# Skip path of a hybrid SSD and attention layer: from the output projection into the attention lanes, through a ring of row tiles; seven staging tiles for weight rows; POOL takes more of the splits

## The chip, the cores and the metric

The kernel runs on one core of a Trainium2 chip. The metric is the time of one execution on the device in microseconds (us), as a median of runs. A profile is one further execution, recorded by the hardware, and gives every instruction with its start and end.

The engines are named as in the profile: PE (TensorE, matmuls; PEld are its weight loads), DVE (VectorE), ACT (ScalarE), POOL (GpSimd), and SP (SyncE), whose queue issues the DMAs here.

## The reference, cut to what matters

One encoder layer on a sequence of 1024 rows of 1024 numbers. In the reference's own terms:

```python
h = layer_norm(x, ln_emb_g, ln_emb_b)
z, xbc, dt_f, dt_b, q, k, v, g = split(h @ w_in)
y_ssm = rms_norm(bidirectional_ssd(silu(conv(xbc)), dt_f, dt_b) * silu(z))
y_att = rms_norm(diff_attention(q, k, v)) * 0.8 * silu(g)      # 8 heads, 2 softmax maps each
mix = concat(y_ssm, y_att) @ w_out                             # 2048 -> 1024
out = layer_norm(alpha * h + mix, ln_g, ln_b)
```

The skip path is the term `alpha * h`. With the mean and the spread of each row of x already known from the first normalisation, it is computed from x again: `(x - mean) * rstd * (alpha * ln_emb_g) + alpha * ln_emb_b`.

## The kernel before

All float32 products are made on PE from halves: a value is split into a rounded high part (a copy on ACT) and a rest (a subtraction on DVE or POOL), and three matmuls take the place of one (high by high, high by low, low by high). Tiles with names in `h` and `l` are such halves: `oh`/`ol` and `or` hold rows of w_out, `oyh`/`oyl` rows of the concatenated y, `whi`/`wlo` columns of w_in, `wh`/`wl` the attention map transposed, `vh`/`vl` the values.

The program is written out by a small planner (`Loom`). Each piece of work is a generator, a *lane*, with a rank in the table `LANES`. At every step the planner takes, of the lanes whose condition holds, the one with the earliest modelled time, then the lowest rank, and at the same rank the one that was added first. PE keeps the order so written; on the other engines the framework places the instructions by the same program order and by what they wait for. Each engine, and the queue of SP, then runs its instructions strictly in its order: what stands behind a waiting instruction waits too.

The stages are: the first normalisation and projections; the SSD groups; eight attention heads (`scores`, `combine`, `values`, `finish`), into which the projections of the next head are filled by the lane `fill`; the last head (head 7), into which the first output projection is filled (`project_out`, part 0: the SSD half of y for eight blocks `tb` of 128 rows); and the output projection's part 1 with the last normalisation. Head 7 has eight blocks `tb` of query rows too; for each, `scores` makes two maps on PE, DVE adds the distance penalty and finds the row extreme, ACT makes the two exponentials, DVE and ACT scale and combine them, PE transposes the result (`bk<-ident,p`), and for each pair of blocks PE multiplies with the values. For each four blocks, `finish` makes an RMS norm, whose sum of squares is the matmul `osh,ones_r`.

`rows_out` loads the rows of w_out by halves (tile `ws`), splits them (`oh0` to `oh15` and `ol0` to `ol15` for the SSD half, later `or`). `y_out` loads y rows (`ys` from the DRAM tiles `yd`) and splits them. `residuals` makes the skip path in tiles `xr` (half rows of a block, 128x512): load, ACT `Identity` with scale and bias, two multiplications and additions on POOL with the rows `g_e` and `b_e`. It runs for blocks 0 to 4 once the projections are through, and later for 5 to 7. DVE then adds a block's product to its `xr`.

Of the kernel before, what the change touches and what calls it, by code (L numbers as in the profile page):

```python
# [9 lines left out]
F32 = mybir.dt.float32  # L10
# [3 lines left out]
AF = mybir.ActivationFunctionType  # L14
ALU = mybir.AluOpType
# [4 lines left out]
D = 1024  # L20
KB = 8
NCH = 8
# [6 lines left out]
LANES = dict(weights=(0, 0.8), channels=(1, 1.2), steps=(2, 1.6), z_tail=(2, 0.8), conv=(3, 1), v_tail=(3, 0.4), states=(4.4, 0.8), diag=(4.125, 0.6), maps=(4.4, 0.6), gate=(4.375, 0.2), finish=(4.2, 2), scores=(4, 0.8), combine=(4.125, 0.6), values=(4.25, 0.4), fill=(9, 0.8), rows_out=(9, 0.2), y_out=(9, 3), residuals=(9, 2), project_out=(9, 2))  # L29
# [187 lines left out]
def hybrid_layer_kernel(  # L217
# [15 lines left out]
    SP = Engine(loom, nc.sync, "DMA", _dma_cost)  # L233
    x, out = x[0], out[0]
# [15 lines left out]
    def dma(dst, src):  # L250
        SP.dma_start(dst, src)

# [113 lines left out]
    zd = [dr.tile([NCH, 128, 512], F32, name=f"zd{g}") for g in range(2)]  # L366

# [98 lines left out]
    def z_block(g, j, when=None):  # L466
        def evac(half, ps):
# [3 lines left out]
            def tail():  # L471
# [6 lines left out]
                dma(zd[g][4 * half:4 * half + 4, :, 128 * j:128 * j + 128].rearrange("c p n -> p c n"), zs)  # L478
# [430 lines left out]
    def proj_k(h):  # L909
        H = heads_[h]  # L910

        def evac(half, ps):
# [4 lines left out]
            for m in range(2):  # L917
# [3 lines left out]
                dma(H.kk[b, m, t].bitcast(F32), H.kk[a, m, t].bitcast(F32))  # L921
# [111 lines left out]
    def values():  # L1033

        for _ in range(64):
# [20 lines left out]
            if tb % 4 == 1:  # L1056
                H.o = ap.tile([128, 512], F32, name="o", bufs=2)
# [46 lines left out]
    for lane in (scores, combine, values):  # L1104
        loom.add(lane())
# [31 lines left out]
    def rows_out():  # L1137
# [5 lines left out]
        def load():  # L1143
            k, n = order[len(sts)]
            sts.append(ap.tile([128, 512], F32, name="ws", bufs=3))
            dma(sts[-1], w_out[128 * k:128 * k + 128, 512 * n:512 * n + 512])
        for _ in range(3):
            load()
        for places in (early_rows(), late_rows()):
            for p in places:  # L1150
# [6 lines left out]
                (V if n else P).tensor_sub(lo, st, hi.bitcast(F32))  # L1157
# [9 lines left out]
    def y_out():  # L1167

        for tb, part in units:
# [5 lines left out]
            for i in range(2):  # L1175
# [5 lines left out]
                V.tensor_sub(lo, st, hi.bitcast(F32))  # L1181
# [3 lines left out]
    res = {}  # L1185
# [3 lines left out]
    def residuals():  # L1189

        yield lambda: "pool" in res
        for n, src in (("g", ln_emb_g), ("b", ln_emb_b)):
            res[n] = res["pool"].tile([128, D], F32, name=n + "_e")
            dma(res[n], src.partition_broadcast(128))
            A.activation(res[n], res[n], AF.Copy, scale=ALPHA)
        late = [("zr", 2), ("zr", 2), ("o", 2), ("o", 2), ("osq", 1), ("msq", 1)]
        for tb in range(8):
# [6 lines left out]
            nmr = ap.tile([128, 1], F32, name="nmr", bufs=2)  # L1204
            V.scalar_tensor_tensor(nmr, mv[tb][:, 0:1], -1.0, rstd[tb], op0=ALU.mult, op1=ALU.mult)
            for n, t in enumerate(halves):
# [5 lines left out]
                dma(xr[n], x[128 * tb:128 * tb + 128, t])  # L1212
# [105 lines left out]
```

## Time and profile before

| | us |
|---|---|
| median of 3 runs | 1235.04 (1233.83 to 1236.17) |
| profiled execution: its own time | 1237.79 |
| profiled execution: span from first to last instruction | 1236.1 |
| busy in the span: PE, DVE, ACT, POOL | 1177.5, 903.5, 702.8, 472.6 |
| mean granted clock of PE | 0.989 |

The span is what the profile's times of instructions lie in, from 0 to 1236.1; 1.7 us of the execution lie outside it. [...] In a timeline row, the bracket at the end tells how long the engine stood idle just before, and what ended that.

### The profile page before, as it was taken

How to read it: one execution, taken by the hardware profiler on the slowest of the kernel's cores; microseconds unless marked ns; L12 is line 12 of the kernel's file. 1: busy time of each engine (PE TensorE's matmuls, PEld its weight loads, DVE VectorE, ACT ScalarE, POOL GpSimd, SP SyncE). 2: the span in 40 equal slices, each digit the busy share in tenths (PEclk: the TensorE clock that was granted, in tenths of full speed). 3: DMA queues.
4: the chain of work that ended last, by engine and by line, in shares of the span. 5: the costliest groups of instructions: out<-in, count | busy, mean ns of one | idle time of the engine just before them, and what ended most of it. 6: DMA issues, size and time to landing. Idle time of an engine off the chain costs nothing. (4 is left out here: it accounts for less than half of the span.)

```text
span 1236.1 us, 16491 instructions
## 1 busy us (share of the span) xinstructions
PE 1177.5 (95%) x5881; PEld 923.5 (75%) x5881; DVE 903.5 (73%) x1303; ACT 702.8 (57%) x1281; POOL 472.6 (38%) x404
## 2 busy tenths in 40 slices
PE   5999999899989999999999999999999998999997
PEld 3777667788667777778787777878778776778885
DVE  6686876767875568788788887887878889952334
ACT  4557478734468456565655657556655686641221
POOL 7412564322753223323232333233232429541354
PEclk9999999999999999999999999999999999989999
DMA  6113236522345521011111121121111262233221
GB/s 198 34 32 116 81 110 173 181 65 53 99 118 149 151 63 43 26 46 50 26 48 39 43 53 26 34 52 36 43 36 42 86 225 83 74 103 114 77 86 60
DMA packets 107592, 98.04 MB, mean 79 GB/s; under 512 B 9364, under 2 KB 79349, under 8 KB 107509
## 3 DMA queue, kind: packets, MB, share of 16 engines
q1 hardware_dynamic: 107509, 96.98, 27.4%
q8 instruction: 46, 0.75, 0.3%
q14 instruction: 37, 0.30, 0.1%
HBM read 75.85 MB, written 16.91 MB: 75 GB/s over the span
## 5 line engine op out<-in xcount | busy, mean ns | idle before, releaser
L140 PE MATMUL bk<-hh,whi 128*128 128x512 f32 x832 | 353.8, 425 | 1.3 <-DVE yt L140 0.7
L140 PE MATMUL bk<-hl,whi 128*128 128x512 f32 x832 | 328.1, 394 | 3.3 <-POOL hl L140 3.0
L140 PE MATMUL bk<-hh,wlo 128*128 128x512 f32 x832 | 328.9, 395 | 0.0
L140 POOL TENSOR_TENSOR wlo<-wst,whi 128x512 fp32r<-128x512 f32 x104 | 160.4, 1546 | 145.1 <-ACT whi L140 129.0
L140 ACT ACTIVATE p<-p,nm 128x1024 f32<-128x1024 f32 x128 | 146.8, 1148 | 121.3 <-DVE nm L140 120.6
L140 POOL TENSOR_SCALAR p<-p,rs 128x1024 f32<-128x1024 f32 x56 | 64.5, 1152 | 350.1 <-DVE rs L140 300.4
L140 PEld LDWEIGHTS bk<-hh,whi 128*128 128x128 f32 x832 | 158.3, 190 | 33.8 <-issue 5.7
L140 PEld LDWEIGHTS bk<-hh,wlo 128*128 128x128 f32 x832 | 157.2, 189 | 35.3
L140 PEld LDWEIGHTS bk<-hl,whi 128*128 128x128 f32 x832 | 158.3, 190 | 33.2 <-POOL hl L140 5.5
L140 DVE CUSTOM_DVE_ANT_0 p<-sc,dist 128x1024 f32<-128x1024 f32 x128 | 151.3, 1217 | 11.9 <-PE sc L140 11.2
L140 DVE SCALAR_TENSOR_TENSOR p<-p,rs,p 128x1024 f32<-128x1024 f32 x64 | 127.8, 1997 | 22.6 <-POOL p L140 18.0
L140 DVE TENSOR_TENSOR wl<-bk,wh 128x512 fp32r<-128x512 f32 x128 | 86.9, 683 | 16.1 <-ACT wh L140 14.2
L140 ACT CAST wh<-bk 128x512 fp32r<-128x512 f32 x128 | 74.1, 579 | 43.1 <-PE bk L140 42.4
L140 ACT CAST whi<-wst 128x512 fp32r<-128x512 f32 x104 | 64.0, 621 | 44.4 <-PE bk L140 37.5
L140 PE MATMUL bk<-ident,p 128*128 128x128 f32 x512 | 79.9, 279 | 4.7 <-DVE wl L140 3.0
L140 PEld LDWEIGHTS bk<-ident,p 128*128 128x128 f32 x512 | 61.9, 142 | 29.5 <-DVE wl L140 6.5
L140 ACT ACT_TABLE_LOAD x46 | 59.0, 1283 | 27.9 <-DVE t L140 17.2
L140 PE MATMUL bk<-wh,vh 128*128 128x256 f32 x256 | 74.6, 291 | 0.0
L140 PE MATMUL bk<-wl,vh 128*128 128x256 f32 x256 | 72.2, 282 | 0.9 <-DVE wl L140 0.9
L140 PE MATMUL sc<-kk,q 128*128 128x512 f32 x256 | 72.4, 394 | 0.0
L140 PE MATMUL bk<-wh,vl 128*128 128x256 f32 x256 | 72.0, 281 | 0.0
L140 PEld LDWEIGHTS bk<-xt,t 128*128 128x128 f32 x256 | 44.9, 189 | 24.3 <-issue 15.8
(217 smaller groups left out, 2168.3 us busy)
## 6 DMA issues: line engine op xcount, KB each, us to landing
wst<-in_w_in_dram SPq DMA_DIRECT2D x104, 256.0 KB, 3.0
t<-acs_d SPq DMA_DIRECT2D x64, 256.0 KB, 3.4
ws<-in_w_out_dram SPq DMA_DIRECT2D x32, 256.0 KB, 3.1
ys<-yd SPq DMA_DIRECT2D x32, 256.0 KB, 3.1
xb<-in_x_dram SPq DMA_DIRECT2D x8, 512.0 KB, 6.3
zd<-zs SPq DMA_DIRECT2D x16, 256.0 KB, 3.0
gz<-zd SPq DMA_DIRECT2D x16, 256.0 KB, 3.1
yd<-ys SPq DMA_DIRECT2D x16, 256.0 KB, 2.5
```

The lines of the kernel that those rows point to most:

```text
L140: r = f(*args, **kw)
```

## The change

- A new lane `skip_rows` (rank 9, added behind `fill`) makes the skip path for all eight blocks. It works in 16 half-row tiles `xe` of 128x512 (first the left halves of blocks 0 to 7, then the right halves). Tile pair i may be written once the counter `o_turn` of the heads' output tiles has passed i + 1. The tiles come from the ring of the heads' output tiles `o`, which has four places in place of two. Each tile is loaded (SP), scaled (ACT), multiplied and added to (POOL), and stored to a DRAM tile `xrd` (SP); a store is written into the program two tiles later. `g_e` and `b_e` are half rows of 128x512, one buffer each, loaded once for the left and once for the right halves.
- `residuals` only loads `xr` from `xrd`. The rows `ln_g` and `ln_b` have tiles of their own and are loaded first.
- `ws` has seven places in place of three.
- The subtraction for `ol` is POOL's for all of the first eight row pairs (before, odd ones were DVE's); the one for `oyl` is POOL's in part 0 (before, DVE's).
- The stores of `zs` (16) and the copies of `kk` (32) are issued on ACT's queue in place of SP's.
- A scratch size for DMAs that the program itself starts is set; the kernel has no such DMA from POOL.

```diff
--- before.py
+++ after.py
@@ -26,7 +26,7 @@
 EPS = 1e-5
 ALPHA = 2.0 ** 0.25
 
-LANES = dict(weights=(0, 0.8), channels=(1, 1.2), steps=(2, 1.6), z_tail=(2, 0.8), conv=(3, 1), v_tail=(3, 0.4), states=(4.4, 0.8), diag=(4.125, 0.6), maps=(4.4, 0.6), gate=(4.375, 0.2), finish=(4.2, 2), scores=(4, 0.8), combine=(4.125, 0.6), values=(4.25, 0.4), fill=(9, 0.8), rows_out=(9, 0.2), y_out=(9, 3), residuals=(9, 2), project_out=(9, 2))
+LANES = dict(weights=(0, 0.8), channels=(1, 1.2), steps=(2, 1.6), z_tail=(2, 0.8), conv=(3, 1), v_tail=(3, 0.4), states=(4.4, 0.8), diag=(4.125, 0.6), maps=(4.4, 0.6), gate=(4.375, 0.2), finish=(4.2, 2), skip_rows=(9, 2), scores=(4, 0.8), combine=(4.125, 0.6), values=(4.25, 0.4), fill=(9, 0.8), rows_out=(9, 0.2), y_out=(9, 3), residuals=(9, 2), project_out=(9, 2))
 
 
 def col_bcast(ap, n):
@@ -231,6 +231,7 @@
     VO = Engine(loom, nc.vector, "DVE", _dve_cost, pinned=True)
     AO = Engine(loom, nc.scalar, "ACT", _act_cost, pinned=True)
     SP = Engine(loom, nc.sync, "DMA", _dma_cost)
+    AD = Engine(loom, nc.scalar, "DMA", _dma_cost)
     x, out = x[0], out[0]
     w_in, w_out, conv_w = w_in[0], w_out[0], conv_w[0]
 
@@ -249,6 +250,10 @@
 
     def dma(dst, src):
         SP.dma_start(dst, src)
+
+    def dma_act(dst, src):
+
+        AD.dma_start(dst, src)
 
     def transpose(dst, src, n=128):
         T.transpose(dst, src, ident[:n, :n])
@@ -364,6 +369,7 @@
     y_dram = [dr.tile([128, 16, 128], F32, name=f"yd{k}") for k in range(8)]
     acs_dr = [dr.tile([16, NCH, 128], F32, name=f"acs_d{d}") for d in range(2)]
     zd = [dr.tile([NCH, 128, 512], F32, name=f"zd{g}") for g in range(2)]
+    xr_dram = [dr.tile([128, D], F32, name=f"xrd{b}") for b in range(NCH)]
 
 
     g0x = px.enter_context(ExitStack())
@@ -475,7 +481,7 @@
                     transpose(pt[:, i, :], zr[:, 128 * i:128 * i + 128])
                 zs = late["sq"].tile([128, 4, 128], F32, name="zs", tag="zr", bufs=2)
                 A.activation(zs, pt, AF.Silu)
-                dma(zd[g][4 * half:4 * half + 4, :, 128 * j:128 * j + 128].rearrange("c p n -> p c n"), zs)
+                dma_act(zd[g][4 * half:4 * half + 4, :, 128 * j:128 * j + 128].rearrange("c p n -> p c n"), zs)
                 G[g].z_done += 1
             loom.add(tail(), "z_tail")
         queue.append(Block(Z0 + 512 * g + 128 * j, evac, when))
@@ -918,7 +924,7 @@
                 a, b = slice(64 * m, 64 * m + 64), slice(64 - 64 * m, 128 - 64 * m)
                 A.copy(H.kk[a, m, t], ps[a])
                 V.tensor_sub(H.kl[a, t], ps[a], H.kk[a, m, t].bitcast(F32))
-                dma(H.kk[b, m, t].bitcast(F32), H.kk[a, m, t].bitcast(F32))
+                dma_act(H.kk[b, m, t].bitcast(F32), H.kk[a, m, t].bitcast(F32))
             H.k += 1
         queue.append(Block(K0 + 128 * h, evac, free_since(h, "scored", 8)))
 
@@ -1054,7 +1060,8 @@
                 continue
             yield lambda: H.v == 2
             if tb % 4 == 1:
-                H.o = ap.tile([128, 512], F32, name="o", bufs=2)
+                H.o = ap.tile([128, 512], F32, name="o", bufs=4)
+                o_turn[0] += 1
             po = bank()
             yield (wl, H.vl, po)
             for s in range(NCH):
@@ -1101,7 +1108,44 @@
     for h in range(1, 8):
         project_head(h)
     queue[-2].pair = queue[-1].last = True
-    for lane in (scores, combine, values):
+    resid = {}
+    o_turn = [0]
+
+    def skip_rows():
+
+
+
+        left = []
+
+        def store():
+            dst, t = left.pop(0)
+            dma(dst, t)
+
+        for i in range(8):
+            yield lambda: o_turn[0] > i + 1
+            for j in range(2):
+                n, tb = i // 4, 2 * (i % 4) + j
+                t = slice(512 * n, 512 * n + 512)
+                if tb == 0:
+                    for name, src in (("g", ln_emb_g), ("b", ln_emb_b)):
+                        resid[name] = ap.tile([128, 512], F32, name=name + "_e")
+                        dma(resid[name], src[t].partition_broadcast(128))
+                        A.activation(resid[name], resid[name], AF.Copy, scale=ALPHA)
+                if len(left) > 1:
+                    store()
+                xe = ap.tile([128, 512], F32, name="xe", tag="o", bufs=4)
+                dma(xe, x[128 * tb:128 * tb + 128, t])
+                nmr = ap.tile([128, 1], F32, name="nmr", bufs=2)
+                V.scalar_tensor_tensor(nmr, mv[tb][:, 0:1], -1.0, rstd[tb], op0=ALU.mult, op1=ALU.mult)
+                A.activation(xe, xe, AF.Identity, scale=rstd[tb], bias=nmr)
+                P.tensor_mul(xe, xe, resid["g"])
+                P.tensor_add(xe, xe, resid["b"])
+                left.append((xr_dram[tb][:, t], xe))
+        while left:
+            store()
+
+    res = {}
+    for lane in (scores, combine, values, skip_rows):
         loom.add(lane())
 
 
@@ -1142,9 +1186,9 @@
 
         def load():
             k, n = order[len(sts)]
-            sts.append(ap.tile([128, 512], F32, name="ws", bufs=3))
+            sts.append(ap.tile([128, 512], F32, name="ws", bufs=7))
             dma(sts[-1], w_out[128 * k:128 * k + 128, 512 * n:512 * n + 512])
-        for _ in range(3):
+        for _ in range(7):
             load()
         for places in (early_rows(), late_rows()):
             for p in places:
@@ -1154,7 +1198,7 @@
                 k, n = order[sum(len(w) for w in wo)]
                 st, (hi, lo) = sts[2 * k + n], p
                 A.copy(hi, st)
-                (V if n else P).tensor_sub(lo, st, hi.bitcast(F32))
+                (V if n and k > 7 else P).tensor_sub(lo, st, hi.bitcast(F32))
                 wo[k].append(p)
                 if len(sts) < 32:
                     load()
@@ -1178,22 +1222,20 @@
                 hi = wp.tile([128, 4, 128], F32R, name="oyh", tag="whi", bufs=4)
                 lo = wp.tile([128, 4, 128], F32R, name="oyl", tag="wlo", bufs=4)
                 A.copy(hi, st)
-                V.tensor_sub(lo, st, hi.bitcast(F32))
+                (V if part else P).tensor_sub(lo, st, hi.bitcast(F32))
                 parts.append((hi, lo))
             ahead[tb, part] = parts
 
-    res = {}
     used = set()
     halves = [slice(0, 512), slice(512, 1024)]
 
     def residuals():
 
         yield lambda: "pool" in res
-        for n, src in (("g", ln_emb_g), ("b", ln_emb_b)):
-            res[n] = res["pool"].tile([128, D], F32, name=n + "_e")
-            dma(res[n], src.partition_broadcast(128))
-            A.activation(res[n], res[n], AF.Copy, scale=ALPHA)
-        late = [("zr", 2), ("zr", 2), ("o", 2), ("o", 2), ("osq", 1), ("msq", 1)]
+        for n, src in (("g", ln_g[0]), ("b", ln_b[0])):
+            res[n + "o"] = res["pool"].tile([128, D], F32, name=n + "_o")
+            dma(res[n + "o"], src.partition_broadcast(128))
+        late = [("zr", 2), ("zr", 2), ("o", 4), ("o", 4), ("o", 4), ("o", 4)]
         for tb in range(8):
             yield lambda: tb < len(used) + 2 or tb > NE
             if tb == NE:
@@ -1201,22 +1243,14 @@
             if tb > NE:
                 yield lambda: last.done == 2
             xr = []
-            nmr = ap.tile([128, 1], F32, name="nmr", bufs=2)
-            V.scalar_tensor_tensor(nmr, mv[tb][:, 0:1], -1.0, rstd[tb], op0=ALU.mult, op1=ALU.mult)
             for n, t in enumerate(halves):
                 if tb < NE:
                     xr.append(res["pool"].tile([128, 512], F32, name=f"xr{tb}_{n}"))
                 else:
                     tag, bufs = late[2 * (tb - NE) + n]
                     xr.append(ap.tile([128, 512], F32, name="xr", tag=tag, bufs=bufs))
-                dma(xr[n], x[128 * tb:128 * tb + 128, t])
-                A.activation(xr[n], xr[n], AF.Identity, scale=rstd[tb], bias=nmr)
-                P.tensor_mul(xr[n], xr[n], res["g"][:, t])
-                P.tensor_add(xr[n], xr[n], res["b"][:, t])
+                dma(xr[n], xr_dram[tb][:, t])
             res[tb] = xr
-        for n, src in (("g", ln_g[0]), ("b", ln_b[0])):
-            res[n + "o"] = res["pool"].tile([128, D], F32, name=n + "_o", tag=n + "_e")
-            dma(res[n + "o"], src.partition_broadcast(128))
 
     def norm_out(tb, xr, po, final):
         st = ap.tile([128, 2, 6], F32, name="bst", bufs=2)
@@ -1303,7 +1337,8 @@
     import concourse.bacc as _bacc
     from concourse.bass_utils import run_bass_kernel_spmd as _run
 
-    nc = _bacc.Bacc("TRN2", target_bir_lowering=False, num_devices=1)
+    nc = _bacc.Bacc("TRN2", target_bir_lowering=False, num_devices=1,
+                     dynamic_dma_scratch_size=512)
     arrays, args = {}, []
     for name in _INS:
         a = _np.ascontiguousarray(inputs[name])
```

The order in which the instructions come to stand shows more than the diff. On POOL, where the last `ol` of the SSD half of w_out are made in head 7, before (the numbers behind names tell tiles of one name apart):

```order
L140 TENSOR_TENSOR ol4_9217<-ws_9202,oh4_9216 128x512
L140 TENSOR_SCALAR p0_8918<-p0_8918,rs_8975 128x1024
L140 TENSOR_TENSOR ol6_9229<-ws_9214,oh6_9228 128x512
L140 TENSOR_TENSOR ol8_9241<-ws_9226,oh8_9240 128x512
L140 TENSOR_TENSOR o_8925<-o_8925,gate_8304 128x512
L140 TENSOR_TENSOR ol10_9253<-ws_9238,oh10_9252 128x512
L140 TENSOR_TENSOR ol12_9265<-ws_9250,oh12_9264 128x512
L140 TENSOR_TENSOR ol14_9277<-ws_9262,oh14_9276 128x512
L140 TENSOR_TENSOR xr0_0_9372<-xr0_0_9372,g_e_9364 128x512
L140 TENSOR_TENSOR xr0_0_9372<-xr0_0_9372,b_e_9367 128x512
```

And now, up to `ol9`:

```order
L140 TENSOR_TENSOR xe_9247<-xe_9247,g_e_9194 128x512
L140 TENSOR_TENSOR xe_9247<-xe_9247,b_e_9197 128x512
L140 TENSOR_TENSOR xe_9255<-xe_9255,g_e_9194 128x512
L140 TENSOR_TENSOR xe_9255<-xe_9255,b_e_9197 128x512
L140 TENSOR_TENSOR ol8_9397<-ws_9358,oh8_9396 128x512
L140 TENSOR_TENSOR xe_9269<-xe_9269,g_e_9262 128x512
L140 TENSOR_TENSOR xe_9269<-xe_9269,b_e_9265 128x512
L140 TENSOR_TENSOR xe_9277<-xe_9277,g_e_9262 128x512
L140 TENSOR_TENSOR xe_9285<-xe_9285,g_e_9262 128x512
L140 TENSOR_TENSOR xe_9277<-xe_9277,b_e_9265 128x512
L140 TENSOR_TENSOR xe_9285<-xe_9285,b_e_9265 128x512
L140 TENSOR_TENSOR ol9_9403<-ws_9364,oh9_9402 128x512
```

Before, POOL made the even `ol` one behind the other (the odd ones were DVE's), and all multiplications of the skip path stood behind them. Now eleven of the sixteen `xe` tiles stand ahead of `ol9`: 9200, 9207 and 9215 behind `ol7`, then the first `oyl`, 9223 and 9231, the second `oyl`, 9239 with the gating of a head's output `o`, and the rows shown.

On PE, the place where `ol8` and `ol9` are first used, before (`sc` are the scores of block 3 of head 7):

```order
L140 MATMUL bk_9312<-ol8_9241,oyh_9296 128x512
L140 MATMUL bk_9313<-ol9_9247,oyh_9296 128x512
L140 MATMUL bk_9312<-oh8_9240,oyl_9297 128x512
L140 MATMUL bk_9313<-oh9_9246,oyl_9297 128x512
L140 MATMUL bk_9312<-oh10_9252,oyh_9296 128x512
L140 MATMUL bk_9313<-oh11_9258,oyh_9296 128x512
L140 MATMUL bk_9312<-ol10_9253,oyh_9296 128x512
L140 MATMUL bk_9313<-ol11_9259,oyh_9296 128x512
L140 MATMUL bk_9312<-oh10_9252,oyl_9297 128x512
L140 MATMUL bk_9313<-oh11_9258,oyl_9297 128x512
L140 MATMUL sc_9413<-kk_8664,q_8472 128x512 x2
```

And now:

```order
L140 MATMUL bk_9468<-ol8_9397,oyh_9452 128x512
L140 MATMUL bk_9469<-ol9_9403,oyh_9452 128x512
L140 MATMUL bk_9468<-oh8_9396,oyl_9453 128x512
L140 MATMUL bk_9469<-oh9_9402,oyl_9453 128x512
L140 MATMUL sc_9545<-kk_8672,q_8480 128x512 x2
L140 MATMUL sc_9548<-kk_8672,q_8480 128x512 x2
L140 MATMUL sc_9545<-kl_8673,q_8480 128x512
L140 MATMUL sc_9548<-kl_8673,q_8480 128x512
```

Up to the second row shown, with `ol9`, the rows of PE are the same in both programs, row by row from the start. Behind it the pieces of the first output projection come later than before, and the scores earlier: scores of block 3, the values of blocks 0 and 1, the transposes of block 2, scores of 4, transposes of 3, scores of 5, the values of 2 and 3, transposes of 4, with no piece of the projection among them.

On ACT, around the exponentials of block 4 of head 7 (`p0_9626`, `p1_9629`), before (there they are `p0_9571`, `p1_9574`):

```order
L140 ACTIVATE xr4_0_9866<-xr4_0_9866,nmr_9864,rstd4_96 128x512
L140 CAST wh_9474<-bk_9545 128x4x128
L140 ACTIVATE xr4_1_9871<-xr4_1_9871,nmr_9864,rstd4_96 128x512
L140 ACTIVATE xr_10002<-xr_10002,nmr_10000,rstd5_97 128x512
L140 ACTIVATE xr_10007<-xr_10007,nmr_10000,rstd5_97 128x512
L140 CAST wh_9474<-bk_9577 128x4x128
L140 ACTIVATE p0_9571,ls_9560<-p0_9571,nm_9559 128x1024
L140 ACTIVATE p1_9574,ls_9560<-p1_9574,nm_9559 128x1024
```

And now:

```order
L140 ACTIVATE p0_9555<-p0_9555,rs_9609 128x1024
L140 COPY o_9561<-bk_9562 128x256
L140 ACTIVATE xe_9317<-xe_9317,nmr_9319,rstd6_98 128x512
L140 CAST wh_9594<-bk_9603 128x4x128
L140 ACTIVATE xe_9325<-xe_9325,nmr_9327,rstd7_99 128x512
L140 CAST wh_9594<-bk_9633 128x4x128
L140 CAST wh_9594<-bk_9640 128x4x128
L140 ACTIVATE p0_9626,ls_9615<-p0_9626,nm_9614 128x1024
L140 ACTIVATE p1_9629,ls_9615<-p1_9629,nm_9614 128x1024
```

Both have scalings of the skip path ahead of the exponentials; now they are those of the last two `xe` tiles. The first `xe` tile stands on ACT behind all exponentials of head 6 and ahead of the first of head 7, so all sixteen lie in head 7. On SP, the loads of `xe_9223` and `xe_9231`, the fourth and fifth tile, stand behind the stores of the first three tiles, and the load of `xe_9317`, the fifteenth, behind the stores of the twelfth to fourteenth (9293, 9301, 9309). The loads of the second `g_e` and `b_e` stand behind the store of the seventh tile (9247).

## Rows read from the trace of the kernel before

**Rows 1.** Windows: start:end, length, busy of PE, PEld, DVE, ACT, POOL, clock, DMA.

```profile
440.00:980.00 540.00, 538.11 (x2898) 425.47 (x2895) 436.09 (x647) 331.05 (x576) 168.44 (x124) 1.00 0.16 41
980.00:1100.00 120.00, 108.67 (x553) 85.98 (x552) 98.42 (x139) 83.34 (x138) 59.95 (x41) 0.96 0.39 123
1005.60:1105.00 99.40, 90.23 (x444) 71.37 (x444) 81.31 (x109) 65.61 (x106) 56.90 (x39) 0.95 0.37 115
1100.00:1228.30 128.30, 128.28 (x554) 103.76 (x552) 48.43 (x83) 28.93 (x45) 55.54 (x45) 1.00 0.28 88
```

**Rows 2.** The chain that ended last, its end: start us, us, what.

```profile
1086.29 30.52 PE bk L140 x136
...
1172.22 56.08 PE bk L140 x240
...
1228.32 0.70 DVE xr L140
```

**Rows 3.** Timeline of PE in the last head: start us, us, instruction.

```profile
1005.66 0.40 PE L140 MATMUL bk<-osh,ones_r 128*128 128x512 f32 x1
...
1014.16 0.70 PE L140 MATMUL bk<-oh,oyh 128*128 128x512 f32 x2
...
1017.02 1.08 PE L140 MATMUL sc<-kk,q 128*128 128x512 f32 x4
1018.03 0.73 PE L140 MATMUL sc<-kl,q 64*128 64x512 f32 x4
...
1029.96 0.51 PE L140 MATMUL bk<-oh,oyh 128*128 128x512 f32 x1 [3.98 <-DVE xr L140]
...
1086.29 1.11 PE L140 MATMUL bk<-ident,p 128*128 128x128 f32 x4 [2.87 <-DVE wl L140]
```

**Rows 4.** Windows of 20 us in the last head, columns as in group 1.

```profile
1020.00:1040.00 20.00, 15.11 (x70) 12.19 (x69) 18.18 (x23) 15.34 (x25) 18.09 (x12) 0.91 0.36 112
1040.00:1060.00 20.00, 18.77 (x100) 14.06 (x99) 18.87 (x26) 13.69 (x22) 19.61 (x14) 1.00 0.09 26
```

**Rows 5.** Timeline of POOL from head 6's end on.

```profile
984.96 1.12 POOL L140 TENSOR_SCALAR p<-p,rs 128x1024 f32<-128x1024 f32 x1 [1.75 <-DVE rs L140]
986.65 1.30 POOL L140 TENSOR_TENSOR ol<-ws,oh 128x512 fp32r<-128x512 f32 x1 [0.56 <-ACT oh L140]
...
1025.61 1.28 POOL L140 TENSOR_TENSOR xr<-xr,g_e 128x512 f32<-128x512 f32 x1
...
1031.66 3.51 POOL L140 TENSOR_TENSOR xr<-xr,b_e 128x512 f32<-128x512 f32 x2
```

**Rows 6.** Groups of instructions from 980 to 1100 us: busy us, mean ns.

```profile
L140 ACT ACTIVATE p<-p,nm 128x1024 f32<-128x1024 f32 x18 | 20.6, 1146 | 7.8 <-DVE nm L140 7.8
L140 DVE SCALAR_TENSOR_TENSOR p<-p,rs,p 128x1024 f32<-128x1024 f32 x10 | 17.7, 1767 | 5.6 <-ACT p L140 4.5 <-POOL p L140 1.0
L140 DVE TENSOR_TENSOR oyl<-ys,oyh 128x512 fp32r<-128x512 f32 x12 | 14.0, 1170 | 0.0
L140 ACT ACTIVATE xr<-xr,nmr,rstd 128x512 f32<-128x512 f32 x13 | 10.0, 808 | 3.0 <-DVE nmr L140 1.6 <-DMA xr<-in_x_dram 1.4
L140 DVE TENSOR_TENSOR ol<-ws,oh 128x512 fp32r<-128x512 f32 x7 | 7.1, 1011 | 0.8 <-ACT oh L140 0.8
L140 ACT ACT_TABLE_LOAD x1 | 1.3, 1283 | 0.0
L140 ACT ACTIVATE g_e<-g_e 128x1024 f32<-128x1024 f32 x1 | 1.1, 1062 | 0.0
```

**Rows 7.** DMA issues of the whole run: count, KB each, median us from issue to landing.

```profile
ws<-in_w_out_dram SPq DMA_DIRECT2D x32, 256.0 KB, 3.1
...
yd<-ys SPq DMA_DIRECT2D x16, 256.0 KB, 2.5
...
xr<-in_x_dram SPq DMA_DIRECT2D x16, 256.0 KB, 5.4
```

**Rows 8.** Tile `oyl`: its instructions on DVE, ns min/median/max.

```profile
L140 DVE TENSOR_TENSOR oyl<-ys,oyh x32: 674/692/1783, 993.0 to 1206.4; 128x512 fp32r<-128x512 f32 x32
```

**Rows 9.** Waits from 100 to 440 us: total us, times, longest.

```profile
PE bk L140 <- DVE t L140: 3.5, 4, 1.3
```

## The prediction

> **What bounds the kernel now.** I read the windows by stage first. In the attention stage PE is busy for 538.11 of 540 us, and in the output projection for 128.28 of 128.30; only the last head leaves PE idle, 99.40 - 90.23 = 9.2 us between 1005.6 and 1105 [rows 1]. The clock granted in those 99.4 us is 0.95, so about 5% of the 90.23 busy us, 4.5 us, are lost to running at half speed behind a stall. The reader is to see that nothing but PE's lost time in the last head can be won there: 9.2 + 4.5 = 13.7 us. The chain that ended last says the same from the other end: from 1086.29 PE runs without a gap to the last addition at 1228.32 [rows 2]. The timeline of PE names the two long waits: 3.98 us for DVE's addition to `xr` before 1029.96, and 2.87 us for DVE's `wl` before 1086.29 [rows 3]. Who is late behind them is seen in the windows of 20 us: DVE is busy for 18.18 and 18.87 of 20, POOL for 18.09 and 19.61 [rows 4]. Both are full there.
>
> **What the change must be judged by.** Both programs issue the same matmuls, and PE's rows are the same up to the first use of `ol9`. So the change in time is PE's lost time from there on, less the 13.7 us.
>
> **Removed.** 8 `ol` and 16 `oyl` leave DVE: 8 x 1.01 + 16 x 1.17 = 27 us at this stage's means [rows 6]. I take it that DVE then no longer holds PE, and count the whole 13.7 us as gone.
>
> **Added, first: the wait for `ol9`.** Before, PE came to the piece with `ol8` and `ol9` at 1014.16 [rows 3], and `ol9` was DVE's. In the new order `ol9` is POOL's, behind eleven `xe` tiles. I follow POOL with 1.28 us for an operation on 128x512 [rows 5]:
>
> - The scaling of the map at 984.96 ends at 986.1; three `ol` of 1.30 [rows 5] end at 990.0. Seven `ws` places let these come early, so I grant that the first three tiles are loaded by then. Six operations: 997.7. The first `oyl`: 999.0.
> - The load of tile 4 stands on SP behind the store of tile 3, which waits for POOL at 997.7. With 0.4 us for the issue and 3.1 for the landing (the median for `ws` of the same size; `xr` took 5.4) [rows 7], and 0.81 on ACT [rows 6], POOL gets tile 4 at 1002.0. Tiles 4 and 5 and the second `oyl`: 1008.4. Tile 6 and a gating: 1012.2. The loads of 7 and 8 were free to go when tiles 4 and 5 were stored, so I count only work: 1017.4. `ol8`: 1018.7.
> - The second `g_e` and `b_e` have one buffer, so their loads wait for tile 8's use of the first, to 1017.4. Issue and landing take them to 1020.9. On ACT they stand behind the gate's activation with two table loads (2 x 1.28 + 1.06) and two exponentials (2 x 1.15) [rows 6], and take half of 1.06 each; I put tile 9 at POOL at 1025. Three tiles of two operations, 7.7, and `ol9`, 1.3: about 1034.
>
> So PE waits from about 1014.2 to 1034, 20 us. From below: with every load hidden, POOL's own work from 999.0 (8 tiles by 2, one `oyl`, one gating, `ol8`, `ol9`) is 20 x 1.28 = 25.6, to 1024.6, and the wait 10 us. From above: where DVE runs beside it, two operations took 3.51 [rows 5], 1.75 each, and 20 of them 9.4 us more: 30 us. ACT's exponentials of block 1, which stand behind tiles 4 and 5, are late too, but PE's delay from that ends inside this wait. I take 18, between the middle and the walk, as some of my landings may be shorter (2.5 for `yd` [rows 7]).
>
> **Added, second: the exponentials of block 4.** On ACT they stand behind the scalings of tiles 15 and 16. Their loads stand behind the store of tile 14. From `ol9`, POOL has six `ol`, two `oyl` and three tiles, 14 x 1.28 = 17.9; issue, landing and two scalings add 0.4 + 3.1 + 1.6: 23 us behind `ol9`. Without that, PE reaches the scores of block 4 about 8 us behind `ol9` (six matmuls of the projection, two scores of 1.8 each [rows 3], values and transposes in between), and ACT could start some 3 us later. That is 12 us late. The transposes of block 4 need the result, and no piece of the projection stands in between. Bounds: 0, if those loads are ahead of POOL, and 13. I take 10.
>
> **Added, third.** In that stretch PE has only scores, transposes and values, and the way from scores to transposes is ACT's two exponentials (2.3), a scaling (1.15) and DVE's combination (1.77) [rows 6] at least. I take 4 us for it over all blocks, between 0 and 8. Half clock behind two longer stalls: each stall behind which it was seen cost about half of the 4.5 us; I take 3 in all, as a wait may swallow part of it, between 1 and 5.
>
> **Nothing or little.** POOL's eight odd `ol` at the end of head 6 lie in its idle time (POOL is busy for 168 of 540 us [rows 1]). The stores of `zs` no longer stand ahead of the loads of `t` on SP: PE waits for DVE's `t` in all 3.5 us between 100 and 440 [rows 9]; I take -1, between -3.5 and +6 for the 48 DMAs that ACT now issues at some 0.4 us each, of which the 32 of `kk` lie under attention, where ACT is busy for 331 of 540 us [rows 1]. The trace shows no DMA that ACT issues, so this is bounded by the waits alone. The reloads of `xr` I count at nothing: the additions that need them stand behind 48 matmuls of each block, and a reload is one landing, 3.1 us by [rows 7]; uncovered, one would cost that.
>
> **The sum.** 18 + 10 + 4 + 3 - 13.7 - 1 = +20. On the profiled execution, 1237.8, that is 1258; it lies 2.75 above the median of the runs, 1235.04, so the forecast for the median is 1255.
>
> [...] `oyl`, whose two inputs lie in SBUF, took 692 ns as a median and 1783 at most [rows 8]; in the last head, where POOL is full, its mean is 1170 [rows 6]. [...]
>
> **The rivals.**
>
> - *Faster: DVE was the bound.* DVE is at 94% in the window from 1040 [rows 4] and both long waits name it [rows 3]. If the tiles run ahead so that `ol9` is there when PE comes, the 13.7 us are won and nothing is lost: 1235 - 14 = 1221. Against it: POOL's order. It decides whether `ol9` ends by about 1015; POOL's work alone ends at 1024.6. A half of it, with a wait of 5 us, would give about 1228. Chance 0.10 for both.
> - *No change.* The second wait is absent and the first at its lower bound: 10 + 4 + 1 - 14 - 1 = 0, 1235. For it: the loads may be ahead of POOL. Chance 0.05.
> - *Later still: POOL and DVE block each other.* With 1.75 for 1.28, the first wait is 30, the second stays: 30 + 10 + 4 + 3 - 14 - 1 = +32, 1267. For it: the pairs of 3.51 us [rows 5]. Against: DVE has 27 us less to do there. Chance 0.20.
> - *My forecast*: 1255, by itself 1243 to 1263. Chance 0.65.
>
> **The numbers.** Faster by over 0.2% (2.5 us, about what a measurement of this kernel can tell from no change): 0.10; within: 0.05; slower: 0.65 + 0.20 = 0.85. The range that leaves out no more than 2 in 10 reaches from 1240 (all of the first rivals and the lowest part of mine below it) to 1270.
>
> **What would show it.** Right: a wait of PE of 10 us or more before a matmul of `oh,oyh` or `ol,oyh` near 1015 to 1035, ended by POOL's `ol` (or the `xe` ahead of it); POOL's `xe` operations in groups of three tiles with idle time ended by ACT or a DMA between; a second wait of some 10 us before transposes (`ident,p`) near 1050 to 1065; a granted clock of 0.5 behind each; from the last RMS matmul on, PE without a gap. Wrong: PE busy through 1015 to 1035, DVE's waits gone, and the last head shorter than before. My prediction is wrong if SP runs the loads of `xe` well ahead of POOL, or if the transposes of block 4 do not wait.

## The result, and the profile after

The changed kernel took 1268.26 us as a median (1266.28 to 1272.05, four runs), the kernel before 1234.53: 33.7 us more, a ratio of 1.0274 with a 95% interval of 1.0255 to 1.0293. That is in the range I gave (1240 to 1270) and on the side I forecast. It is 13 us above the forecast itself, and above the 1243 to 1263 that I gave the forecast by itself: only the third rival's number, 1267, lies near it. The profiled execution took 1267.73 us, with a span of 1266.0.

The windows of the changed kernel, columns as in [rows 1]:

```profile
440.00:980.00 540.00, 538.60 (x2914) 428.71 (x2913) 439.82 (x650) 336.70 (x582) 181.94 (x127) 1.00 0.18 45
980.00:1100.00 120.00, 87.30 (x403) 64.70 (x402) 77.48 (x119) 78.33 (x129) 81.84 (x61) 0.82 0.56 184
1006.46:1036.00 29.54, 12.91 (x47) 8.76 (x47) 15.51 (x25) 23.57 (x37) 23.58 (x18) 0.72 0.72 239
1036.00:1068.00 32.00, 21.07 (x82) 14.29 (x81) 19.48 (x27) 14.44 (x24) 25.47 (x19) 0.61 0.52 171
1068.00:1114.80 46.80, 43.36 (x230) 34.60 (x229) 32.32 (x46) 28.82 (x51) 19.37 (x14) 1.00 0.40 127
1114.80:1258.30 143.50, 143.50 (x620) 116.42 (x620) 42.42 (x79) 25.04 (x38) 51.36 (x43) 1.00 0.23 68
```

The attention stage is as full as before [rows 1]. In the last head PE is idle for 16.6, 10.9 and 3.4 us in the three windows from 1006 to 1115 (each length less its busy time), 31.0 in all, where it was 9.2 before. Its granted clock (PE's clock in the profile, as a share of full speed) is 0.72 and 0.61 in the first two of them, where it was 0.95 before [rows 1]. From the last RMS matmul at 1114.80 PE runs through. The timeline of PE, the rows with its waits:

```profile
1009.52 0.80 PE L140 MATMUL bk<-osh,ones_r 128*128 128x512 f32 x1 [3.06 <-ACT osh L140]
1012.92 0.80 PE L140 MATMUL bk<-osl,ones_r 128*128 128x512 f32 x1 [2.60 <-DVE osl L140]
...
1029.62 0.80 PE L140 MATMUL bk<-oh,oyh 128*128 128x512 f32 x1 [6.38 <-ACT oh L140]
...
1035.42 0.79 PE L140 MATMUL bk<-ol,oyh 128*128 128x512 f32 x1 [4.58 <-POOL ol L140]
...
1047.82 1.09 PE L140 MATMUL bk<-ident,p 128*128 128x128 f32 x4 [4.38 <-DVE p L140]
1052.53 1.12 PE L140 MATMUL bk<-ident,p 128*128 128x128 f32 x4 [3.62 <-DVE wl L140]
...
1057.76 1.12 PE L140 MATMUL bk<-ident,p 128*128 128x128 f32 x4 [1.25 <-ACT o L140]
1060.50 1.12 PE L140 MATMUL bk<-ident,p 128*128 128x128 f32 x4 [1.63 <-DVE wl L140]
...
1070.28 0.63 PE L140 MATMUL bk<-ident,p 128*128 128x128 f32 x4 [0.98 <-DVE rs L140]
```

The two long waits of before [rows 3] are gone, and eight others of over 1 us stand there up to 1062; the transposes of 1047.82 and 1052.53 are those of block 2, the next two those of block 3, and those at 1070.28 are block 4's. What the waits stood for is seen on ACT, DVE and POOL. On ACT (timeline):

```profile
1001.51 1.66 ACT L140 ACTIVATE xe<-xe,nmr,rstd 128x512 f32<-128x512 f32 x2 [6.62 <-DMA xe<-in_x_dram]
...
1004.06 1.15 ACT L140 ACTIVATE p<-p,nm 128x1024 f32<-128x1024 f32 x1
...
1028.24 0.81 ACT L140 ACTIVATE xe<-xe,nmr,rstd 128x512 f32<-128x512 f32 x1 [1.39 <-DVE nmr L140]
1028.96 3.72 ACT L140 CAST oh<-ws 128x512 fp32r<-128x512 f32 x7
...
1046.56 0.81 ACT L140 ACTIVATE xe<-xe,nmr,rstd 128x512 f32<-128x512 f32 x1 [4.89 <-DVE nmr L140]
...
1047.79 1.15 ACT L140 ACTIVATE p<-p,nm 128x1024 f32<-128x1024 f32 x1
...
1057.33 0.37 ACT L140 COPY o<-bk 128x256 f32<-128x256 f32 x1 [5.13 <-DMA xrd<-xe]
```

ACT waited 6.62 us for the load of the fourth tile, with block 1's exponentials behind it; the `oh` come behind the eleventh tile's scaling; the exponentials at 1047.79 behind the fourteenth's; and a head's output `o` waited 5.13 us for a tile of the shared ring to be stored. PE's wait of 4.38 us before 1047.82 was ended by DVE's combination of block 2's maps, which stood right behind a `nmr` of 3.62 us (timeline of DVE; more on that one in the last section):

```profile
1042.85 3.62 DVE L140 SCALAR_TENSOR_TENSOR nmr<-mv,rstd 128x1 f32<-128x1 f32 x1
1046.40 1.27 DVE L140 SCALAR_TENSOR_TENSOR p<-p,rs,p 128x1024 f32<-128x1024 f32 x1
```

On POOL, from the fourth tile and to `ol9`:

```profile
1002.40 1.30 POOL L140 TENSOR_TENSOR xe<-xe,g_e 128x512 f32<-128x512 f32 x1 [3.23 <-ACT xe L140]
...
1026.22 1.65 POOL L140 TENSOR_TENSOR xe<-xe,g_e 128x512 f32<-128x512 f32 x1 [5.72 <-ACT xe L140]
...
1034.07 8.72 POOL L140 TENSOR_TENSOR ol<-ws,oh 128x512 fp32r<-128x512 f32 x7
```

I had the fourth tile on POOL at 1002.0, the ninth at 1025 and `ol9` done at 1034; it began at 1034.07.

### The profile page after: what moved, and what is told of

Its sections match the earlier page's. It is cut to its first block, busy times and chain, and to the rows that moved or that the text cites. A ratio compares the mean times of both kernels' runs of the same rounds, so it can differ in the third digit from the quotient of the medians.

```text
span 1266.0 us, 16477 instructions
## 1 busy us (share of the span) xinstructions
PE 1182.9 (93%) x5881; PEld 927.8 (73%) x5881; DVE 889.6 (70%) x1287; ACT 705.5 (56%) x1283; POOL 508.6 (40%) x428
## 4 chain that ended last, share of the span: by engine, by line
PE 58%; DVE 17%; ACT 7%; DMA 5%; POOL 4%; issue 4%; SPq 1%; DVEq 0%; ACTq 0%; POOLq 0%
PE bk L140 46%; PE sc L140 9%; DVE p L140 4%; ACT p L140 3%; PE sb L140 3%; DVE yt L140 2%; POOL xe L140 2%; DMA gz<-zd 1%; DVE t L140 1%; DVE xc L140 1%; POOL p L140 1%; DVE osl L140 1%; SPq L140 1%; DMA xe<-in_x_dram 1%; ACT t L140 1%
## 5 line engine op out<-in xcount | busy, mean ns | idle before, releaser
L140 POOL TENSOR_TENSOR wlo<-wst,whi 128x512 fp32r<-128x512 f32 x104 | 167.0, 1610 | 131.3 <-ACT whi L140 114.9
L140 DVE SCALAR_TENSOR_TENSOR p<-p,rs,p 128x1024 f32<-128x1024 f32 x64 | 119.4, 1865 | 14.1 <-POOL p L140 10.1
L140 PEld LDWEIGHTS bk<-ident,p 128*128 128x128 f32 x512 | 61.6, 143 | 40.6 <-issue 10.6
L140 PE MATMUL sc<-kk,q 128*128 128x512 f32 x256 | 75.8, 409 | 0.0
```

The lines of the kernel that those rows point to most:

```text
L140: r = f(*args, **kw)
```

## The experiments

Theory: the harm is the place. The skip tiles stand in the last head, each load behind the store of an earlier tile, and ACT and POOL, in order, hold back `oh9`, `ol9` and the exponentials. Rival A: POOL's added splits. Rival B: the skip path's added traffic and POOL work cost wherever they stand. In the code shown, `...` marks lines left out. Each ratio is to the kernel before on the same chip, with its interval.

**Another place: the lane's rank 4.5 for 9** (one entry of the table `LANES`).

```diff
-skip_rows=(9, 2)
+skip_rows=(4.5, 2)
```

> The changed kernel with one number altered: the rank of the lane of the skip rows is 4.5 in place of 9, so that its tiles stand under heads 1 to 5 and none in the last head; the work is the same. Theory (the harm is the place: tiles in the last head, whose loads wait for stores and which hold POOL and ACT ahead of ol9 and of the exponentials): the waits of PE of 6.4 and 4.6 us before the second quarter of the first projection piece, and those of 4.4 and 3.6 us before transposes, are gone; 1222 to 1233 us, faster than the kernel before. Rival A (POOL's added splits are the harm): about 1262 to 1270 still. Rival B (the extra 8.4 MB through memory and the queue, and POOL working beside DVE, cost wherever they stand): 1236 to 1250.

Measured: 1244.03 us, ratio 1.0080 (1.0053 to 1.0106). The same work, with its scalings now between 508 and 775 us under the earlier heads, costs 24 us less than in the last head, and the waits for `oh9` and `ol9` are gone. But it is not faster than before: my number was missed, and the size is that of rival B. Two windows, columns as in [rows 1]:

```profile
440.00:980.00 540.00, 528.59 (x2820) 421.21 (x2820) 414.69 (x632) 339.71 (x583) 211.23 (x156) 0.99 0.22 62
980.00:1100.00 120.00, 109.39 (x571) 84.62 (x570) 88.82 (x135) 73.69 (x124) 45.59 (x33) 0.97 0.32 99
```

PE lost 11.4 us in the window under the heads (1.9 before [rows 1]), and 10.6 in the next 120 us, nearly the 11.3 of before. Among the waits there, ACT's for the tiles' loads:

```profile
ACT xe L140 <- DMA xe<-in_x_dram: 6.7, 4, 4.4
```

**The splits given back to DVE, tiles left in the last head.**

```diff
-(V if n and k > 7 else P).tensor_sub(lo, st, hi.bitcast(F32))
+(V if n else P).tensor_sub(lo, st, hi.bitcast(F32))
...
-(V if part else P).tensor_sub(lo, st, hi.bitcast(F32))
+V.tensor_sub(lo, st, hi.bitcast(F32))
```

> The changed kernel with the subtractions for the odd ol and for oyl of part 0 given back to DVE, as before; the skip tiles stay in the last head. Theory: oh9 still stands on ACT behind the scaling of the eleventh tile and the exponentials of block 4 behind the fifteenth and sixteenth, so most of the loss stays: 1252 to 1268 us, with a wait before the same piece ended by ACT's oh in place of POOL's ol. Rival A (POOL's added splits are the harm): 1230 to 1240.

Measured: 1257.31 us, ratio 1.0189 (1.0159 to 1.0220). Two thirds of the loss stay, and the wait for the same piece is now ended by ACT, as expected (timeline of PE in this run):

```profile
1027.41 0.80 PE L140 MATMUL bk<-oh,oyh 128*128 128x512 f32 x1 [10.01 <-ACT oh L140]
```

**All but the skip path.** The kernel before with the seven staging tiles, the splits on POOL, the DMAs on ACT's queue and the scratch size:

```diff
-name="ws", bufs=3
+name="ws", bufs=7
...
-(V if n else P).tensor_sub(lo, st, hi.bitcast(F32))
+(V if n and k > 7 else P).tensor_sub(lo, st, hi.bitcast(F32))
...
-V.tensor_sub(lo, st, hi.bitcast(F32))
+(V if part else P).tensor_sub(lo, st, hi.bitcast(F32))
...
-dma(H.kk[b, m, t].bitcast(F32), H.kk[a, m, t].bitcast(F32))
+dma_act(H.kk[b, m, t].bitcast(F32), H.kk[a, m, t].bitcast(F32))
```

> The kernel before with all parts of the change except the skip path: seven staging tiles, POOL's splits, the stores of zs and the copies of kk on ACT's queue, the scratch size. Theory: no long wait for ol9 (ahead of it on POOL stand only splits and one gating), 1226 to 1238 us. Rival A: about 1262 to 1270, as POOL then has the splits and the skip path of the output projection in the same 60 us. The long wait for DVE's addition to xr may grow, as xr stands on POOL behind the splits.

Measured: 1229.11 us, ratio 0.9951 (0.9936 to 0.9965): faster than before. Rival A falls: without the move of the skip path, POOL's splits do no harm. The loss needs the skip path; a third of it, 11 us (1268 against 1257 in the run before this one), needs POOL's splits behind the tiles as well.

**Rank 4.5 with the splits on DVE** (the two edits above together).

> As the run with rank 4.5, with the subtractions for the odd ol and for oyl of part 0 back on DVE. It tells what the splits are worth where POOL is free. Theory: without the skip path in the last head DVE still has 27 us more of subtractions there; 2 to 10 us slower than with rank 4.5 alone, 1228 to 1238. Rival A: faster than with rank 4.5 alone.

Measured: 1251.70 us, ratio 1.0142 (1.0114 to 1.0170), 7.7 above the run with rank 4.5 alone: the difference is the one I expected, the time itself is not, as it was reckoned from a run that came out slower. Where POOL is not held by skip tiles, the splits on it are a gain; in the last head, behind the tiles, the same splits cost 11 us (1268 against 1257).

**The biases made ahead.** Eight `nmr`, once, in place of sixteen:

```diff
+        nmrs = []
+        for tb in range(8):
+            nmrs.append(ap.tile([128, 1], F32, name=f"nmr{tb}"))
+            V.scalar_tensor_tensor(nmrs[tb], mv[tb][:, 0:1], -1.0, rstd[tb], op0=ALU.mult, op1=ALU.mult)
...
-                A.activation(xe, xe, AF.Identity, scale=rstd[tb], bias=nmr)
+                A.activation(xe, xe, AF.Identity, scale=rstd[tb], bias=nmrs[tb])
```

> The changed kernel with the eight biases nmr (128x1) of the skip tiles computed once at the head of the lane, into tiles of their own, in place of one by one beside POOL's stream. In the changed kernel's trace one of them lasted 3.62 us on DVE beside three operations of POOL in a row, ACT waited 4.9 us for another, and PE then 4.4 and 3.6 us for the transposes. Theory (DVE's small operation, blocked by POOL's stream, is on the path of that second wait): 1259 to 1264 us. Rival (the tiles' loads and POOL are late anyway): 1266 to 1270.

Measured: 1272.83 us, ratio 1.0315 (1.0283 to 1.0347). ACT no longer waits for `nmr`, and nothing is won, so the theory of the second wait has no support. It is not a clean test: PE's order came out otherwise, with its waits at other pieces, ended by ACT's `oyh` and POOL's `oyl` (timeline of PE):

```profile
1037.49 1.22 PE L140 MATMUL bk<-oh,oyh 128*128 128x512 f32 x2 [10.37 <-ACT oyh L140]
1047.75 1.22 PE L140 MATMUL bk<-oh,oyl 128*128 128x512 f32 x2 [8.18 <-POOL oyl L140]
```

**A ring of its own for the tiles** (and six staging tiles, and other places for the last `xr`, for room).

```diff
-xe = ap.tile([128, 512], F32, name="xe", tag="o", bufs=4)
+xe = ap.tile([128, 512], F32, name="xe", bufs=3)
...
-H.o = ap.tile([128, 512], F32, name="o", bufs=4)
+H.o = ap.tile([128, 512], F32, name="o", bufs=2)
```

> The changed kernel with a ring of its own for the skip tiles (three places), two places for the heads' outputs, and six staging tiles for room; no other line. In the built order all sixteen tiles then stand under head 0, so it is the shared ring that holds them back to the last head. Theory (the place in the last head is the harm): the waits before the first projection's second quarter are gone; 1224 to 1236 us, with new waits of PE of some us between 440 and 500, where ACT waits for the tiles' loads. Rival (the skip tiles cost the same wherever they stand): 1255 to 1268.

Measured: 1243.05 us, ratio 1.0074 (1.0046 to 1.0102). Without the shared ring all sixteen tiles ran between 440 and 516 us: it was the ring, taken in the order of the heads' outputs, that held them back. The loss of the last head is gone (PE busy for 115.42 of the 120 us from 980 to 1100, 108.67 before [rows 1]), the waits under head 0 are more than I thought (PE busy for 528.42 of the 540 us under attention), and the time lies between theory and rival.

**Rank 4.5, biases ahead, and loads awaited.** A wait in the planner between load and scaling, so that other work is written ahead of the scaling until the load should have landed:

```diff
                 dma(xe, x[128 * tb:128 * tb + 128, t])
+                yield xe
```

> As the run with rank 4.5 (1244 us), with the biases made ahead and the planner told to wait for a tile's load before it writes the tile's scaling. Theory (in that run ACT, in order, waited 6.7 us for the tiles' loads, and PE lost 11 us under the heads): 1232 to 1240. Rival (it is the work of ACT and POOL itself, beside DVE, that costs under the heads): 1242 to 1246.

Measured: 1230.67 us, ratio 0.9977 (0.9958 to 0.9995), a little faster than before, 13 us faster than rank 4.5 alone, and below the 1232 to 1240 that I expected. ACT's waits for the loads fell from 6.7 to 0.5 us (waits from 440 to 980):

```profile
ACT xe L140 <- DMA xe<-in_x_dram: 0.5, 1, 0.5
```

The biases and the awaited loads were not tried apart at this rank.

**Staging tiles and queues alone**: the run of all but the skip path, with the splits back on DVE.

> The run of all but the skip path (1229 us) with the subtractions for the odd ol and for oyl of part 0 back on DVE: seven staging tiles and DMAs on ACT's queue alone are left of the change. Theory (DVE, 94% busy, held PE, and the splits were its relief): 1233 to 1238. Rival (the staging tiles or the queues gave those 6 us): 1227 to 1231.

Measured: 1232.77 us, ratio 0.9993 (0.9978 to 1.0008): no change. So the gain of 1229 comes with the splits, some 4 to 5 us of it.

**The tiles' arithmetic on DVE**, from the run with awaited loads:

```diff
-                P.tensor_mul(xe, xe, resid["g"])
-                P.tensor_add(xe, xe, resid["b"])
+                V.tensor_mul(xe, xe, resid["g"])
+                V.tensor_add(xe, xe, resid["b"])
```

> As the run with early tiles and awaited loads (1231 us), with the multiplication and the addition of each skip tile on DVE in place of POOL. That run still lost 9.6 us of PE under the heads, 8 more than the kernel before, in waits of under 1 us for the most part. [...] Rival (DVE is full under the heads, 436 of 540 us before, and 22 us more of work delay the maps): 1231 to 1240.

Measured: 1252.19 us, ratio 1.0157 (1.0128 to 1.0186). It is 21.5 us above the run with these operations on POOL. The rival is right in kind and too small (1231 to 1240): the two operations of a tile took 683 and 688 ns on DVE as medians (tile `xe`), 22 us for sixteen tiles, and PE under the heads was busy for 523.26 of 540 us, where it was 530.43 with them on POOL. Its waits there name DVE:

```profile
PE bk L140 <- DVE p L140: 5.4, 4, 2.5
PE bk L140 <- DVE wl L140: 5.2, 4, 2.8
```

**The tiles spread over heads 1 to 6**, from the same run:

```diff
-            yield lambda: o_turn[0] > i + 1
+            yield lambda: o_turn[0] > 1 + 3 * i // 2
```

> As the run with early tiles and awaited loads (1231 us), with the tiles spread over heads 1 to 6 in place of 1 to 4 (a pair for every one and a half output tiles). Theory (each tile costs some half microsecond under the heads by its two POOL operations, wherever it stands): 1229 to 1232, no change. Rival (it is their crowding, several tiles behind one another ahead of a needed operation): 1224 to 1228.

Measured: 1221.98 us, ratio 0.9905 (0.9880 to 0.9929), the fastest of all, some 1% faster than the kernel before and below the range of either side. It holds four edits together: the rank, the biases ahead, the awaited loads and the spreading. Its windows, columns as in [rows 1]:

```profile
440.00:980.00 540.00, 535.34 (x2890) 427.64 (x2889) 433.92 (x647) 347.47 (x599) 219.98 (x158) 1.00 0.22 60
980.00:1100.00 120.00, 118.55 (x630) 95.29 (x629) 83.34 (x124) 76.28 (x130) 57.08 (x40) 1.00 0.41 130
```

PE loses 4.7 us under the heads, 9.6 with the tiles crowded into heads 1 to 4, and 1.5 in the 120 us in which it lost 11.3 before [rows 1]. That fits the crowding, as the rival said.

**Transfers alone in the last head.** The biases, the scalings and POOL's two operations are left out; the output lacks the normalisation of the skip path.

```diff
-                nmr = ap.tile([128, 1], F32, name="nmr", bufs=2)
-                V.scalar_tensor_tensor(nmr, mv[tb][:, 0:1], -1.0, rstd[tb], op0=ALU.mult, op1=ALU.mult)
-                A.activation(xe, xe, AF.Identity, scale=rstd[tb], bias=nmr)
-                P.tensor_mul(xe, xe, resid["g"])
-                P.tensor_add(xe, xe, resid["b"])
```

> The changed kernel with the biases, the scaling on ACT and the two operations on POOL of the skip tiles left out: x is loaded, stored and reloaded through the ring in the last head as it is, so the output lacks the normalisation of the skip path. Theory (the loss is made of ACT and POOL standing in order behind tiles whose loads are late): with nothing of theirs behind the loads PE's waits go, 1226 to 1236. Rival (the extra 8.4 MB, or SP's queue with stores ahead of the loads of w_out, hold PE): 1250 to 1268.

Measured: 1229.35 us, ratio 0.9962 (0.9946 to 0.9977). So the added traffic and SP's order by themselves do not make the loss: this is as fast as the kernel without the skip path's move (1229.11). That does not show them free. The arithmetic is gone here, and the run is still some 7 us slower than the one with the tiles spread (1222), which has all of it. PE lost 7.8 of the 120 us, where that one lost 1.5 (window, and timeline of PE):

```profile
980.00:1100.00 120.00, 112.16 (x572) 89.22 (x571) 83.04 (x121) 76.15 (x130) 53.42 (x38) 0.97 0.60 197
```

```profile
1034.49 0.66 PE L140 MATMUL bk<-ident,p 128*128 128x128 f32 x4 [2.78 <-DVE xr L140]
```

The longest wait is for DVE's addition to `xr`. The last store of the tiles was issued at 1023.1 (tile `xe` in this run). That DVE stood for a reload of `xr` is my guess from this and was not shown.

**Without POOL's work on the tiles.** Only the last two of these lines are left out; the skip path lacks `ln_emb_g` and `ln_emb_b`.

> The changed kernel with the multiplication and addition of the skip tiles on POOL left out, so the skip path lacks ln_emb_g and ln_emb_b; loads, scalings on ACT and stores stay in the last head, in nearly the same order on ACT. Transfers alone gave 1229 us. Theory (ACT standing behind scalings whose loads stand behind stores is a good half of the loss, POOL's order the other): 1238 to 1252, with a wait of PE ended by ACT's oh that stays. Rival (POOL's two operations are what makes everything late, the stores and so the loads too): 1227 to 1234.

Measured: 1241.86 us, ratio 1.0063 (1.0039 to 1.0087), 12.5 us above transfers alone. A wait ended by ACT's `oh` stays (timeline of PE):

```profile
1021.46 0.80 PE L140 MATMUL bk<-oh,oyh 128*128 128x512 f32 x1 [4.53 <-ACT oh L140]
```

So of the 39 us between transfers alone and the changed kernel, taken out in this order, the biases and the scalings on ACT bring 12 or 13, and POOL's operations, which also delay the stores and so the loads behind them (in the changed kernel SP's queue stood 44.9 us in all for POOL's `xe` between 980 and 1070 us), the other 26. My split, a half each, was wrong: POOL's is two thirds.

## Why the prediction was right, point by point

- *What bounds it.* Right. PE's lost time in the last head is where the change shows; attention (538.60 of 540 us) and the output projection stayed as they were.
- *Removed, 13.7 us.* Right in kind: the long waits for DVE's `xr` and `wl` are gone from the changed kernel. What they are worth is seen only where nothing takes their place: 1222 us with the tiles spread, 11 us below the kernel before.
- *The wait for `ol9`, 18 us.* Right in place and size, and in the cause that ended it: idle 16.6 us between 1006.46 and 1036, and PE past `ol9` at 1035.42, where I walked to 1034. It came in four pieces, of which two stood at the RMS matmul (ACT's exponentials behind the fourth tile's load) and one was ended by ACT's `oh9`. I had named only POOL for this wait; the run with the splits on DVE shows ACT alone holding PE for 10 us there.
- *The exponentials of block 4, 10 us.* The mechanism failed, and the size agrees by luck. ACT's scaling of tile 16 ended at 1062.1, some 27 us behind `ol9`, where I had 23, so the exponentials of block 4 were as late as I walked, and more. But the transposes of block 4, at 1070.28, waited only 0.98 us, and by my own sign (wrong "if the transposes of block 4 do not wait") this part was wrong. What I had not counted is that PE would be late itself by then: it was idle for 10.9 us from 1036 to 1068 at the transposes of blocks 2 and 3. The first of these waits, 4.38 us, was ended by DVE's combination behind a long `nmr`; the second, 3.62, stood behind block 3's exponentials, which stood on ACT behind tile 14, whose `nmr` was late on DVE; the last two, 1.25 and 1.63, behind a head's output, which waited for its place in the shared ring. I had named none of them.
- *The way from scores to transposes, 4 us.* 3.4 us idle from 1068 to 1114.80, close in size; 0.98 of it is the wait of block 4's transposes.
- *Half clock, 3 us: the term that was mis-sized.* From where PE came to the first RMS matmul of the last head to the last matmul, the kernel before took 1228.3 - 1005.66 = 222.6 us and the changed one 1258.3 - 1006.46 = 251.8, with the same matmuls: 29.2 more, of which 31.0 - 9.2 = 21.8 are idle time. The other 7.4 are clock, on top of the 4.5 of before: 11.9 us, where I put 3, between 1 and 5. The windows say the same: 28% of 12.91 busy us and 39% of 21.07 are 11.8. I priced it per stall, from the stalls of before behind which PE had work without a gap (granted 0.50 from 1032 to 1034 and from 1086 to 1092); here each wait was followed by a short piece of work and the next wait, and the granted clock stood at half (0.50) from 1048 to 1064:

```profile
1048.00:1052.00 4.00, 0.91 (x4) 0.51 (x3) 2.67 (x6) 4.00 (x7) 4.00 (x4) 0.50 0.39 131
1052.00:1056.00 4.00, 3.47 (x12) 2.42 (x12) 2.08 (x2) 0.20 (x1) 4.00 (x3) 0.50 0.17 66
1056.00:1060.00 4.00, 1.62 (x8) 0.72 (x4) 0.25 (x1) 1.66 (x3) 1.12 (x2) 0.50 0.94 273
1060.00:1064.00 4.00, 3.48 (x10) 1.78 (x10) 3.93 (x7) 2.75 (x5) 3.64 (x4) 0.50 0.74 246
```

- *Nothing or little, -1 us.* At the RMS matmul PE was 0.8 us later than before, not earlier. PE's wait for DVE's `t` from 100 to 440 us was 7.8 us, not less than the 3.5 of before [rows 9]; so the stores on ACT's queue did not shorten it. In the changed kernel an issue took 0.37 us (stores of `zs`) and 0.47 us (copies of `kk`) on ACT's queue and 0.38 us (loads of `xe`) on SP's, as medians, where I counted 0.4. The reloads of `xr`, counted at nothing and at 3.1 us if uncovered, landed 5.2 us behind their issue as a median in the changed kernel; none shows as a wait of PE's there; whether one stands behind the 2.78 us with the transfers alone was not shown. Of the eight odd `ol` that I put at the end of head 6, the last four (`ol9`, 11, 13 and 15) stood in head 7, as my other terms have it.
- *The sum.* 31.0 + 11.9 - 13.7 + 0.8 = 30.0; the spans differ by 29.9. Of the missing 10 us of my sum, 9 are the clock.
- *The rivals.* The third, POOL and DVE blocking each other, gave nearly the measured time, but not for its reason: the `xe` operations on POOL had medians of 1.28 and 1.29 us, as I had counted, not 1.75 (rows below, tile `xe` in the changed kernel). Only the long `nmr` on DVE is of its kind. My range reached up to 1270 to take in that rival, so that it held is in part luck: the sum of my own terms was 10 us short. The first rival named the right kind of prize: where the tiles are out of the way, DVE's relief and the lost waits give 1222 us. That its reckoning was 1221 is in part chance, as that run also loses 2.8 us more under the heads than the kernel before.

```profile
L140 POOL TENSOR_TENSOR xe<-xe,g_e x16: 1258/1281/1650, 989.2 to 1062.1; 128x512 f32<-128x512 f32 x16
L140 POOL TENSOR_TENSOR xe<-xe,b_e x16: 1263/1290/2270, 990.6 to 1063.5; 128x512 f32<-128x512 f32 x16
```

## What to carry to other kernels

A lane of "idle-time" work has two places to read before it is judged: the rank that its planner gives it, and the ring that its tiles share; here the two together sent all of it into the stage where DVE and POOL were already full [rows 4] (a change of either took it out again), and the built order showed it before any run. The work that loads, scales and stores through a small ring advanced here as its stores did, and what stood behind it on ACT and POOL was late with it: block 1's exponentials behind ACT's wait of 6.62 us for a tile's load, `ol9` behind POOL's of 5.72 us for a scaled tile; a head's output waited 5.13 us for a tile's store. Here it helped to await the load in the planner and not on the engine (with the biases made ahead, 13 us) and to spread the pieces (9 us more). Price half clock by the whole stretch until PE has work without gaps again, not by the stall: here that made 11.9 us in place of 3.

## What the runs showed of the hardware that I had not expected

The DVE operation `nmr` on 128x1 that began at 1042.85 lasted 3.62 us in the changed kernel (its row stands under the result). The timeline of POOL at that time:

```profile
1042.73 2.51 POOL L140 TENSOR_TENSOR oyl<-ys,oyh 128x512 fp32r<-128x512 f32 x2
1045.18 1.27 POOL L140 TENSOR_TENSOR xe<-xe,g_e 128x512 f32<-128x512 f32 x1
1046.53 2.27 POOL L140 TENSOR_TENSOR xe<-xe,b_e 128x512 f32<-128x512 f32 x1
```

It began 0.12 us behind the start of POOL's pair and ended within 0.02 us of POOL's third operation (1046.45); the shortest of its kind took 0.15 us. That POOL held it is read from these times and was not tried apart. One instruction of DVE so lasted through three of POOL's that followed each other closely. POOL's next operation, which began 0.13 us behind the start of DVE's combination of the maps, lasted 2.27 us, where the median of its kind was 1.29.
